# Hybrid decoder block on one core: other PSUM banks for small sums, a third attention head turned through DRAM, a re-ordered output projection and later residual sums

## The chip, the cores and the metric

The kernel runs on one core of one Trainium2 chip. The metric is device time in microseconds (us) of one execution. Before the change it was timed three times: 2241.65, 2243.55 and 2248.02 us, so the median is 2243.55 us. One further execution was recorded by the profiler; every duration below is from that one.

The engines are named as the profile names them: PE is TensorE's matmul unit and PEld its weight load, DVE is VectorE, ACT is ScalarE, POOL is GpSimd, SP is SyncE (which here only issues DMAs). SBUF is the on-chip memory, PSUM the eight accumulator banks that PE writes.

## The reference

One decoder layer over 512 tokens of width 2048, in float32. What matters here:

```
h = rms_norm(x);  parts = h @ w_in
o_nsa = 8 query heads over compressed, selected and window keys   (nsa_mixer)
o_gla = 4 heads of gated linear attention                         (gla_mixer)
x = x + concat(rms_norm(o_nsa), o_gla) @ w_out

cq = rms_norm(per head of rms_norm(x) @ w_cq)      # 4 heads of 128, 512 tokens
ck, cv = the same of the 256 memory tokens
p = softmax(cq @ ck^T);  x = x + (p @ cv) @ w_co   # cross attention

hf = rms_norm(x);  gg, uu = split(hf @ w_gu)
return x + (silu(gg) * uu) @ w_down                # d_ff = 5632
```

## The kernel before, in words

**Precision.** Every float32 operand is split into a high and a low part (`split`, lines 201 to 207: ACT casts the high part, DVE subtracts to get the low one), and each product is three matmuls, high by high, high by low and low by high (`mm3`, which calls the helper that records every matmul at line 110). A weight tile of 128x1024 elements goes from DRAM to a `w` tile and from there to a `wh` and a `wl` tile. A product of full width (512 columns) follows the one before it on PE after about 0.227 us.

**Order of the work.** The program is traced once and a list scheduler at build time fixes the order of every engine's instructions from a model of their times; at run time each engine takes its instructions in that fixed order and waits on semaphores. Work is written as "flows": generators that run beside the big projections. `flows.tick()` is called after every two 128-row steps of a projection (eight times in a projection of 2048 rows), and `yield n` in a flow puts its next piece n ticks later in the program. `behind(i)` forces the instructions inside it to come after instruction i on its engine. PSUM banks are lent by name: `mm` has three buffers, `s` two, `t` two, `o` one. A tile of SBUF that is lent by name waits in the same way until an earlier holder has been read for the last time.

**The eight heads of the first attention** (`nsa_head`, line 926 on). Each head's query projection (`in_tile`) ends in an `mm` bank. The head takes the squares, sums them (`partial_sums` on DVE, four ticks later `total_sums` at line 937, which takes a PSUM bank for one matmul of 16 columns against a matrix of ones and gives it back when DVE has read it), and works out its scale. Then come eight groups of scores, each in an `s` bank: mm3, a DVE reduction over them (line 1017, its running minimum is the tile `mn`) and an exponential on ACT. When they are done, the weights are turned by PE (line 1072) and multiplied with the values into the `o` bank, in two rounds b = 0 and 1. Head 0 is started just before the projection `natural(w_vsw, ...)` of the values, which holds three `mm` banks and the `o` bank from its start to its end (`natural_end`, which reads them out at lines 206 and 207); the other heads run beside the projections that follow.

**Cross attention** (`cross_head`, line 1198 on). Four projections of w_cq follow each other, and head h starts when projection h is done. Two ticks later (one for the last head) its scores are computed against 256 memory tokens in two `s` banks, then scaled and put through the softmax (lines 1229 to 1239). The weights must be turned so that memory tokens lie on partitions. For heads 0 and 1 DVE turns 32x32 blocks of them (line 1245, two instructions of 128x512), POOL stores the result to DRAM in four DMAs (line 1250) and loads it back in the wanted order in two (line 1253). For heads 2 and 3 PE turns them into a `t` bank by eight matmuls of 128 columns (line 1266). Ten (heads 0, 1), four (head 2) or six (head 3) ticks after the softmax the turned weights are split into the tiles PH and PL (one buffer each), and after that six products with the memory's values go to the one `o` bank and are split into the pair `oc[h]`.

**The projection w_co** (line 1285 on). Its first four output tiles, m = 0 to 3, use the three `mm` banks and one `s` bank. `co_part(ps, m, hs)` adds three products for each head in hs. Before the change the loop ran over m outside and heads 0 to 2 inside, waiting at h = 2 for that head's pair; the products of head 3 of all four tiles follow (line 1322), and only then are the output tiles added to x and the rest of w_co computed.

**The down projection** (line 1780 on). Four steps over 22 pairs of 128 rows of w_down each; step 2 has two sets of four accumulators, `banks[0]` in the banks mm, o, t, t and `banks[1]` in s, s, mm, mm. At its end ACT copies `banks[0]` to SBUF (line 1832) and `pending` asks for eight additions on DVE that read `banks[1]` from PSUM (two result blocks, line 1762); they are put at kp = 1 of step 3, ahead of the new accumulators. Twelve more additions (`spread`) follow one to a kp from kp = 3 on, eight of them followed by the store of a piece of the output.

Of the kernel before, what the change touches and what calls it, by code (L numbers as in the profile page):

```python
# [10 lines left out]
F32 = mybir.dt.float32  # L11
# [52 lines left out]
def hybrid_block(ctx: ExitStack, tc: tile.TileContext, x_t, mem_t, sv, cmat, umask, w_a, w_r67, w_v, w_vg, w_v3,  # L64
# [14 lines left out]
    def sb(shape, tag, bufs, dt=F32):  # L79
        return (pool_b if tag in LATE else pool).tile(shape, dt, name=tag, tag=tag, bufs=bufs)  # L80
# [173 lines left out]
    def mm3(ps, lhs, rhs, start, stop, again=False):  # L254
        mm(ps, lhs[0], rhs[0], start=start, stop=False, skip_group_check=again)
        mm(ps, lhs[0], rhs[1], start=False, stop=False, skip_group_check=again)
        mm(ps, lhs[1], rhs[0], start=False, stop=stop, skip_group_check=again)

    def part(pair, a, n):
        return pair[0][:, a:a + n], pair[1][:, a:a + n]  # L260

    def view(t, at, *dims):
        return bass.AP(tensor=t.tensor, offset=t.offset + at, ap=[list(t.ap[0])] + [list(d) for d in dims])
# [74 lines left out]
    def total_sums(dst, part, tag):  # L338
        ps = bank(tag)
        mm(ps[:, :16], every32, part, start=True, stop=True)  # L340
        p4 = part.rearrange("p (i g) -> p i g", g=4)
        V.tensor_mul(p4, ps[:, :16].rearrange("p (i g) -> p i g", g=4),
                     own32[:, None, :].to_broadcast([128, NT, 4]))
        V.reduce_sum(dst, p4, axis=AX.X)
# [581 lines left out]
    def nsa_head(h, ps):  # L926
# [7 lines left out]
        sc, sl, neg, part_, m3 = qt[:, 0:4], qt[:, 4:8], qt[:, 8:12], qt[:, 12:28], qt[:, 28:29]  # L934
        partial_sums(part_, sq, row("n"))
        yield W_SUM + 1
        total_sums(neg, part_, "s")
        V.tensor_mul(neg, neg, rc2)
        inv_rms(sc, neg, 128, sl)
        V.tensor_mul(sc, sc, rc)  # L940
# [257 lines left out]
    def cross_head(h, ps):  # L1198
        q = row("Q", F32R), row("Q", F32R)
        sq = row("n")  # L1200
        S.activation(sq, ps, AF.Square)
        split(*q, ps, g_cq)
        cf = triple("cf")
        sc, tmp, v = cf[:, 0], cf[:, 1], cf[:, 2]
        if h < 3:
            part_ = small("qs", 2)[:, :16]
            partial_sums(part_, sq, row("n"))
        yield 1 if h == 3 else 2
        if h == 3:
            pn = bank("t")  # L1210
            for i in range(NT):
                mm(pn[:, i:i + 1], sq[:, 128 * i:128 * i + 128], one, start=True, stop=True)
        scores = [bank("s") for _ in range(2)]
        for a in range(2):
            for i in range(2):
                mm3(scores[a][:, MEM * i:MEM * i + MEM], part(q, 128 * (2 * a + i), 128), part(ckp, MEM * h, MEM),
                    start=True, stop=True)
        if h < 3:
            total_sums(v, part_, "t")
        V.tensor_mul(v, v if h < 3 else pn[:, :NT], rc[1])  # L1220
        inv_rms(sc, v, 128, tmp)
        V.tensor_mul(sc, sc, rc[0])
        sm, mn = triple("sm"), triple("mn")
        halves = []
        for a in range(2):
            s = scores[a]
            p = row("e")
            two = slice(2 * a, 2 * a + 2)
            V.tensor_reduce(mn[:, 0, two], s.rearrange("p (i n) -> p i n", i=2), axis=AX.X, op=OP.max, negate=True)
            V.tensor_mul(mn[:, 0, two], mn[:, 0, two], sc[:, two])  # L1230
            for i in range(2):
                j = 2 * a + i
                S.activation(p[:, MEM * i:MEM * i + MEM], s[:, MEM * i:MEM * i + MEM], AF.Exp,
                             bias=mn[:, 0, j:j + 1], scale=sc[:, j:j + 1], accum_out=sm[:, 0, j:j + 1])
            V.reciprocal(mn[:, 1, two], sm[:, 0, two])
            for i in range(2):
                j = 2 * a + i
                pi = p[:, MEM * i:MEM * i + MEM]
                V.tensor_scalar(pi, pi, mn[:, 1, j:j + 1], None, op0=OP.mult)
            halves.append(p)  # L1240
        rows = []
        if h < 2:
            z = sb([128, 1024], "w", 4)
            for a in range(2):
                V.transpose(view(z, 64 * a, (32, 2), (128, 8), (1, 32)), halves[a])
            d = dram.tile([128, 1024], F32, name="crossp", tag="crossp", bufs=2)
            dv = d.rearrange("(c s) (b a x) -> s b c a x", s=32, b=2, a=4)
            zv = z.rearrange("p (b c x) -> p b c x", b=2, c=4)
            for a in range(4):
                G.dma_start(dv[:, :, :, a], zv[32 * a:32 * a + 32])  # L1250
            for b in range(2):
                rows.append(row("st"))
                G.dma_start(rows[b], d[:, 512 * b:512 * b + 512])
        yield 6 if h == 3 else 10 if h < 2 else 4
        pts = []
        for b in range(2):
            pt = sb([128, 1280], ("PH", "PL")[b], PTB, F32R)
            pts.append((pt[:, :512], pt[:, 512:1024]))
            if rows:
                split(*[view(t, 0, (32, 4), (128, 4), (1, 32)) for t in pts[b]],  # L1260
                      rows[b].rearrange("p (a i x) -> p a i x", a=4, i=NT))
                continue
            tp = bank("t")
            for i in range(NT):
                c = MEM * (i % 2) + 128 * b
                PE.transpose(tp[:, 128 * i:128 * i + 128], halves[i // 2][:, c:c + 128], ident)
            split(*pts[b], tp)
        yield 2 if h == 3 else 1
        o = bank("o")
        for b in range(2):  # L1270
            mm3(o, part(cvp[b], 128 * h, 128), pts[b], start=b == 0, stop=b == 1)
        pair = row(OC[h], F32R), row(OC[h], F32R)
        split(*pair, o)
        oc.append(pair)
# [9 lines left out]
    sb([128, 24], "pad", 1)  # L1284
    co = [Weights(w_co[c], 1024, ahead=60) for c in range(2)]
    ps4 = [bank("mm") for _ in range(3)]
    for m in range(4):
        if m == 3:
            ps4.append(bank("s"))
        for h in range(3):  # L1290
            flows.until(lambda: len(oc) > h)
            co_part(ps4[m], m, (h,))
            flows.tick()
    flows.drain()
# [489 lines left out]
    for step, plan in enumerate(STEPS):  # L1784
        rs_ = range(len(plan))
        for kp in range(NK):
            if step or kp % 2 == 0:
                load_w(step, kp)

            if kp == 1:  # L1790
                for s in pending:
                    gather_all(s)
                if step == 0:
                    banks[0] = banks[1]
                elif step == 2:
                    banks[1] = [bank(t) for t in SETS[1]]
                else:
                    banks = [[bank(t) for t in SETS[r]] for r in rs_]
            if kp in (1, NK - 1):
                for r in rs_ if kp == 1 else reversed(rs_):  # L1800
                    for x in range(4):
                        for k in (kp - 1, kp):
                            down_product(step, r, k, (x,))
                        if step == 3 and kp == NK - 1:
                            gather(ADD, *((0, 0), (1, 0))[r], banks[r], x, True)
            elif 1 < kp < NK - 2:
                for r in rs_:
                    down_product(step, r, kp, range(4))
            if kp in ROWS[step]:
                load_rows(*ROWS[step][kp])  # L1810
            if kp in SUMS[step]:
                add_rows(*SUMS[step][kp])
            if step == 0 and kp == 3:
                last_turn = turn(hs, NB - 1)
            if kp >= 3 or step:
                for go in last_turn.get(NK * step + kp, ()):
                    go()
            move_h(step, kp)
            if step == 3 and kp > 2 and spread:
                with behind(*last_split):  # L1820
                    gather(*spread.pop(0))
        if step == 0:
            pending = [(COPY, 0, 1, banks[0])]
            res[0, 1] = new_res(0, 1)
        elif step == 1:
            pending = [(COPY, 0, 0, banks[0]), (COPY, 1, 1, banks[1]), (ADD, 0, 1, banks[1])]
            for a in range(2):
                res[a, a] = new_res(a, a)
        elif step == 2:
            u = quarters(sb2("H"))  # L1830
            for x in range(4):
                S.copy(u[x], banks[0][x])
            pending = [(SUB, 1, 1, banks[1]), (ADD, 1, 0, banks[1])]
            spread = [(*p, x, last) for *p, last in ((SUB, 1, 1, u, True), (SUB, 0, 1, u, True), (ADD, 1, 0, u, False))
                      for x in range(4)]


_OUT = (4, 128, 2048)
# [120 lines left out]
```

## Time and profile before

| | |
|---|---|
| three timed executions | 2241.65, 2243.55, 2248.02 us |
| profiled execution, its own time | 2241.54 us |
| its span, first to last instruction | 2239.8 us |
| granted TensorE clock | 1.000 |
| PE, PEld busy | 2229.3 us, 1851.8 us |
| DVE, ACT, POOL busy | 1709.5 us, 1159.6 us, 299.7 us |
| mean DMA throughput | 200 GB/s |

The profile's page gives busy time by engine, the chain of waits that ended last, and groups of instructions by line. The trace behind it can be asked for windows (busy time and number of instructions, in brackets behind an x, of each engine in a stretch), for waits (who waited for whom), for a timeline of one engine, and for DMAs with their time from issue to landing. Times are counted from the first instruction. PE's matmuls are pipelined and their ends are modelled: the distance between two starts says how long PE was held, and the time in square brackets behind a row is idle time before it with the instruction that ended it.

### The profile page before, as it was taken

How to read it: one execution, taken by the hardware profiler on the slowest of the kernel's cores; microseconds unless marked ns; L12 is line 12 of the kernel's file. 1: busy time of each engine (PE TensorE's matmuls, PEld its weight loads, DVE VectorE, ACT ScalarE, POOL GpSimd, SP SyncE). 2: the span in 40 equal slices, each digit the busy share in tenths (PEclk: the TensorE clock that was granted, in tenths of full speed). 3: DMA queues.
4: the chain of work that ended last, by engine and by line, in shares of the span. 5: the costliest groups of instructions: out<-in, count | busy, mean ns of one | idle time of the engine just before them, and what ended most of it. 6: DMA issues, size and time to landing. Idle time of an engine off the chain costs nothing.

```text
span 2239.8 us, 29015 instructions
## 1 busy us (share of the span) xinstructions
PE 2229.3 (100%) x10404; PEld 1851.8 (83%) x10404; DVE 1709.5 (76%) x2653; ACT 1159.6 (52%) x1715; POOL 299.7 (13%) x453
## 2 busy tenths in 40 slices
PE   9999999999999999999999999999999999999999
PEld 8898888888887888888888888888888888888887
DVE  7648986667878336788889888988888886766786
ACT  7534564556777324575455445544554554454443
POOL 0122221122221220120011101110110011001000
PEclk9999999999999999999999999999999999999999
DMA  8588778965563983595456546554664477768684
GB/s 305 179 220 201 190 188 223 248 172 170 151 169 112 250 229 95 162 265 201 148 184 197 173 150 195 189 170 154 198 201 142 150 281 261 268 241 281 250 278 163
DMA packets 130784, 448.23 MB, mean 200 GB/s; under 512 B 16240, under 2 KB 17520, under 8 KB 127696
## 3 DMA queue, kind: packets, MB, share of 16 engines
q1 hardware_dynamic: 81040, 304.71, 39.8%
q0 software_dynamic: 47152, 137.39, 24.7%
q10 hardware_dynamic: 2448, 4.28, 0.5%
q8 instruction: 81, 1.33, 0.2%
q14 instruction: 63, 0.52, 0.1%
HBM read 401.10 MB, written 107.09 MB: 227 GB/s over the span
## 4 chain that ended last, share of the span: by engine, by line
PE 96%; DVE 2%; DMA 1%; ACT 1%; issue 1%; SPq 0%; DVEq 0%; POOLq 0%; ACTq 0%
PE mm L110 52%; PE t L110 18%; PE s L110 14%; PE o L110 11%; PE t L1072 1%; DMA raw<-gu 0%; DMA raw<-td 0%; DMA PH<-w_ck 0%; DMA ss<-q 0%; DMA ss<-KV 0%; DVE ql L204 0%; DVE e L741 0%; DVE P L1017 0%; DVE wl L204 0%; ACT wh L204 0%
## 5 line engine op out<-in xcount | busy, mean ns | idle before, releaser
L204 ACT CAST qh<-raw 128x1024 fp32r<-128x1024 f32 (+1 forms) x494 | 478.5, 976 | 468.2 <-PE o L110 128.0
L204 DVE TENSOR_TENSOR ql<-raw,qh 128x1024 fp32r<-128x1024 f32 (+1 forms) x494 | 550.6, 1124 | 106.1 <-PE mm L110 40.1
L110 PE MATMUL mm<-X,wh 128*128 128x512 f32 x1664 | 524.4, 394 | 0.0
L110 PEld LDWEIGHTS mm<-X,wh 128*128 128x128 f32 x1664 | 306.4, 188 | 59.1 <-issue 0.8
L110 PE MATMUL t<-qh,PB 128*128 128x512 f32 x968 | 333.0, 389 | 0.0
L110 PE MATMUL mm<-X,wl 128*128 128x512 f32 x832 | 325.6, 392 | 0.5 <-DVE wl L204 0.5
L110 PE MATMUL mm<-qh,PB 128*128 128x512 f32 x868 | 309.1, 389 | 0.1
L204 DVE TENSOR_TENSOR wl<-w,wh 128x1024 fp32r<-128x1024 f32 (+2 forms) x172 | 205.5, 1200 | 130.8 <-ACT wh L204 127.9
L204 ACT CAST wh<-w 128x1024 fp32r<-128x1024 f32 (+2 forms) x172 | 176.8, 1033 | 232.9 <-PE mm L110 151.8
L110 PE MATMUL s<-qh,PB 128*128 128x512 f32 x672 | 231.0, 389 | 0.0
L110 PE MATMUL mm<-qh,PA 128*128 128x512 f32 x640 | 220.0, 389 | 0.0
L110 PEld LDWEIGHTS t<-qh,PB 128*128 128x128 f32 x968 | 181.7, 188 | 37.9
L110 PEld LDWEIGHTS mm<-qh,PB 128*128 128x128 f32 x868 | 163.0, 188 | 34.2 <-ACT qh L204 0.7
L110 PE MATMUL t<-ql,PB 128*128 128x512 f32 x484 | 188.3, 389 | 0.0
L110 PE MATMUL o<-qh,PB 128*128 128x512 f32 x484 | 187.4, 389 | 0.0
L110 PEld LDWEIGHTS mm<-X,wl 128*128 128x128 f32 x832 | 156.2, 188 | 33.9 <-DVE wl L204 1.8
L110 PE MATMUL mm<-ql,PB 128*128 128x512 f32 x434 | 169.3, 390 | 1.1 <-DVE ql L204 1.1
L110 PEld LDWEIGHTS s<-qh,PB 128*128 128x128 f32 x672 | 126.1, 188 | 25.9
L110 PEld LDWEIGHTS mm<-qh,PA 128*128 128x128 f32 x640 | 120.1, 188 | 25.0
L110 PE MATMUL s<-ql,PB 128*128 128x512 f32 x336 | 131.0, 390 | 0.1
L110 PE MATMUL mm<-ql,PA 128*128 128x512 f32 x320 | 124.5, 389 | 0.0
L1424 DVE TENSOR_TENSOR raw<-raw 128x1024 f32<-128x1024 f32 x80 | 97.0, 1223 | 18.8 <-DMA raw<-w_gu 18.4
(534 smaller groups left out, 3493.4 us busy)
## 6 DMA issues: line engine op xcount, KB each, us to landing
raw<-w_gu SPq DMA_DIRECT2D x80, 768.0 KB, 4.2
raw<-w_down SPq DMA_DIRECT2D x88, 512.0 KB, 4.8
raw<-w_gu SPq DMA_DIRECT2D x80, 512.0 KB, 3.6
td<-w_down POOLq DMA_DIRECT2D x66, 512.0 KB, 7.4
w<-w_a SPq DMA_DIRECT2D x60, 512.0 KB, 6.3
raw<-td SPq DMA_DIRECT2D x22, 1024.0 KB, 6.7
w<-w_out SPq DMA_DIRECT2D x32, 512.0 KB, 6.1
HR<-h POOLq DMA_DIRECT2D x28, 512.0 KB, 4.5
```

What stands on the lines that cost most here:

```text
L110: last_mm[0] = PE.matmul(*args, **kw)
L204: last_split[:] = S.copy(hi, src), V.tensor_sub(lo, src, hi)
L1072: PE.transpose(tp[:, 128 * (i - j):128 * (i - j) + 128], ps_[b][:, POFF[i] + 128 * j:POFF[i] + 128 * j + 128], ident)
L1424: V.tensor_add(raw[:, 0:1024], raw[:, 0:1024], raw[:, 512:1536])
```

## The change

There are four edits.

1. `nsa_head`: the small sums' matmul takes an `mm` bank, no longer an `s` bank.
2. `cross_head`: the score matmuls are put behind the matmul last recorded before them; head 2 is turned as heads 0 and 1 are, with nine ticks to its split; and for all three heads the way through DRAM is cut into two halves of 128 memory tokens each: two DVE instructions of 128x256 into a 512 wide tile (`q1` or `rs` in place of a `w` tile), four stores and one load for each half, all eight stores ahead of the two loads.
3. `w_co`: the first four tiles' products go head by head, heads outside and tiles inside.
4. Down projection: at the end of step 2 ACT also copies `banks[1]` to SBUF, nothing is pending at step 3, and the eight additions that read those banks join `spread`, which begins at kp = 1 and has twenty entries; the eight that are followed by a store come at kp = 9 to 16.

```
@@ nsa_head
-        total_sums(neg, part_, "s")
+        total_sums(neg, part_, "mm")
@@ cross_head
-        for a in range(2):
-            for i in range(2):
-                mm3(scores[a][:, MEM * i:MEM * i + MEM], part(q, 128 * (2 * a + i), 128), part(ckp, MEM * h, MEM),
-                    start=True, stop=True)
+        with behind(last_mm[0]):
+            for a in range(2):
+                for i in range(2):
+                    mm3(scores[a][:, MEM * i:MEM * i + MEM], part(q, 128 * (2 * a + i), 128), part(ckp, MEM * h, MEM),
+                        start=True, stop=True)
...
-        if h < 2:
-            z = sb([128, 1024], "w", 4)
-            for a in range(2):
-                V.transpose(view(z, 64 * a, (32, 2), (128, 8), (1, 32)), halves[a])
-            d = dram.tile([128, 1024], F32, name="crossp", tag="crossp", bufs=2)
-            dv = d.rearrange("(c s) (b a x) -> s b c a x", s=32, b=2, a=4)
-            zv = z.rearrange("p (b c x) -> p b c x", b=2, c=4)
-            for a in range(4):
-                G.dma_start(dv[:, :, :, a], zv[32 * a:32 * a + 32])
+        if h < 3:
             for b in range(2):
-                rows.append(row("st"))
-                G.dma_start(rows[b], d[:, 512 * b:512 * b + 512])
-        yield 6 if h == 3 else 10 if h < 2 else 4
+                z = row(("q1", "rs")[b])
+                for a in range(2):
+                    V.transpose(view(z, 64 * a, (32, 2), (128, 4), (1, 32)),
+                                view(halves[a], 128 * b, (MEM, 2), (1, 128)))
+                d = dram.tile([128, 512], F32, name="crossp", tag="crossp", bufs=6)
+                for a in range(4):
+                    G.dma_start(d[:, 128 * a:128 * a + 128].rearrange("(c s) x -> s c x", s=32),
+                                z[32 * a:32 * a + 32].rearrange("s (c x) -> s c x", c=4))
+                rows.append(d)
+            for b in range(2):
+                t = row("st")
+                G.dma_start(t, rows[b])
+                rows[b] = t
+        yield 6 if h == 3 else 10 if h < 2 else 9
@@ w_co
-    for m in range(4):
-        if m == 3:
-            ps4.append(bank("s"))
-        for h in range(3):
-            flows.until(lambda: len(oc) > h)
+    for h in range(3):
+        flows.until(lambda: len(oc) > h)
+        for m in range(4):
+            if len(ps4) == m:
+                ps4.append(bank("s"))
             co_part(ps4[m], m, (h,))
             flows.tick()
@@ down projection
-            if step == 3 and kp > 2 and spread:
+            if step == 3 and kp and spread:
...
-            pending = [(SUB, 1, 1, banks[1]), (ADD, 1, 0, banks[1])]
-            spread = [(*p, x, last) for *p, last in ((SUB, 1, 1, u, True), (SUB, 0, 1, u, True), (ADD, 1, 0, u, False))
-                      for x in range(4)]
+            w = [sb2("PA") for _ in range(4)]
+            for x in range(4):
+                S.copy(w[x], banks[1][x])
+            pending = []
+            spread = [(*p, x, last) for *p, last in ((SUB, 1, 1, w, False), (ADD, 1, 0, w, False), (SUB, 1, 1, u, True),
+                                                     (SUB, 0, 1, u, True), (ADD, 1, 0, u, False)) for x in range(4)]
```

## The prediction, made before the changed kernel was run

> **What bounds the kernel now.** I read the page first, its busy times and the chain of waits:
>
> ```profile
> PE 2229.3 (100%) x10404; PEld 1851.8 (83%) x10404; DVE 1709.5 (76%) x2653; ACT 1159.6 (52%) x1715; POOL 299.7 (13%) x453
> ...
> PE 96%; DVE 2%; DMA 1%; ACT 1%; issue 1%; SPq 0%; DVEq 0%; POOLq 0%; ACTq 0%
> ```
>
> PE bounds the kernel: 96% of the chain that ended last is matmuls. So an edit can win only the holes in PE's row, and it can lose as much as it opens. Busy time hides small holes, because the ends of matmuls are modelled; so I read windows next, for the number of matmuls in the bracket behind PE (first column), then PE's own waits in the three stretches that are touched (360 to 720, 870 to 1010, 1980 to 2240 us):
>
> ```profile
> 448.00:504.00 56.00, 56.00 (x289) 47.43 (x288) 37.94 (x112) 32.03 (x67) 12.86 (x17) 1.00 0.67 171
> 1064.00:1120.00 56.00, 56.00 (x248) 46.36 (x247) 48.44 (x60) 25.22 (x30) 4.33 (x7) 1.00 0.43 148
> 2072.00:2128.00 56.00, 55.13 (x244) 45.33 (x243) 39.98 (x39) 27.66 (x30) 5.34 (x10) 1.00 0.69 250
> ```
> ```profile
> PE s L110 <- DVE mn L1017: 1.0, 4, 0.2
> ```
> ```profile
> PE s L110 <- ACT Q L206: 0.8, 1, 0.8
> ```
> ```profile
> PE mm L110 <- DVE ql L204: 0.9, 1, 0.9
> ```
>
> A stretch of full-width matmuls alone holds 248 in 56 us, 0.226 us each. In the row from 1064 on there is no hole at all; the down projection's 244 is four short, 0.9 us. The three touched stages show waits of 1.0, 0.8 and 0.9 us. That is the purse: a few microseconds of 2240. About 0.3%, 6.7 us, is what a measurement of this kernel can tell from no change, so the prize lies below it, and the question is whether an edit opens a hole larger than that.
>
> **Edit 1, the sums' bank.** The wait on `mn` is the sums' matmul standing for an `s` bank:
>
> ```profile
> 543.06 0.27 PE L110 MATMUL o<-PL,KV 128*128 128x128 f32 x1
> 543.18 0.27 PE L110 MATMUL o<-PH,KV 128*128 128x128 f32 x1
> 543.70 0.37 PE L110 MATMUL s<-qs,every 128*128 128x16 f32 x2 [0.25 <-DVE mn L1017]
> ```
>
> The product at 543.18 holds PE some 0.12 us, as its like at 543.06 did, so 0.40 us are lost. The waits view has four such; a fifth, smaller, without a hole in the busy row I put at 0.2. In an `mm` bank they vanish, since beside one projection in progress and one just read out the third is free: 4 x 0.40 + 0.2 = **1.8 us won**. The transposes behind it and the next scores find their bank at the same time as now, so no wait takes their place for sure (rival 3 prices that).
>
> Head 0 is different. Its sums run while the value projection holds all three `mm` banks:
>
> ```profile
> 388.69 0.29 PE L110 MATMUL s<-qs,every 128*128 128x16 f32 x2
> ...
> 449.70 0.60 PE L1072 MATMUL t<-ident,P 128*128 128x128 f32 x4
> ```
> ```profile
> 436.66 0.75 DVE L207 SCALAR_TENSOR_TENSOR KV<-mm,rc,KV 128x512 fp32r<-128x512 f32 x1
> ```
> ```profile
> 405.44 0.41 DVE L998 TENSOR_SCALAR P<-P,cf 128x384 f32<-128x384 f32 x1
> ```
>
> The sums now come when the first of these banks is read out, about 436.7, 48 us later; head 0's eight groups of scores follow them. Its first round is scaled at 405.9 now, 17.2 us after the sums; at that pace it would be ready at 453.9, 4.2 us after the turning at 449.70 wants it. That pace is set by ticks; without them the groups run as fast as DVE and ACT let them, and the projections of head 1 give PE other work. So 0 to 4.2 us are lost; below nothing there is no reason. I take **1.0**, near the lower end, because DVE has room there (37.94 of 56 us busy from 448 on). Edit 1 is worth -1.8 + 1.0 = -0.8 us.
>
> **Edit 2 and 3, the scores' place.** Head 1's scores stand in front of a projection that was ready:
>
> ```profile
> 894.14 0.61 PE L110 MATMUL mm<-X,wh 128*128 128x512 f32 x2
> 895.57 0.51 PE L110 MATMUL s<-P,Q 128*128 128x256 f32 x2 [0.81 <-ACT Q L206]
> ```
>
> Two products of 0.227 end at 894.59, so 0.98 us are lost. Behind the twelve matmuls recorded before them, 2.7 us of work, the scores come when Q is there: **1.0 us won**, at least 0.5 if the matmuls themselves wait for their weights.
>
> **The third head.** Removed are eight turning matmuls:
>
> ```profile
> 923.00 0.70 PE L1266 MATMUL t<-ident,e 128*128 128x128 f32 x4
> 923.46 0.48 PE L110 MATMUL mm<-X,wl 128*128 128x512 f32 x1
> ```
>
> Four take 0.46, all eight 0.9 us of PE. The way through DRAM takes their place. The rows of heads 0 and 1 give its price:
>
> ```profile
> 906.68 0.70 DVE L1245 STREAM_TRANSPOSE w<-e 128x512 f32<-128x512 f32 x1
> 907.30 0.65 DVE L204 TENSOR_TENSOR PL<-st,PL 128x512 fp32r<-128x512 f32 x1
> ...
> 923.58 0.62 DVE L1239 TENSOR_SCALAR e<-e,mn 128x256 f32<-128x256 f32 x2
> ...
> 948.06 0.42 DVE L1349 TENSOR_TENSOR PB<-PB 128x256 f32<-128x256 f32 x1
> ```
> ```profile
> DMA to landing us min/median/max: 2.4/3.9/4.7
> ```
> ```profile
> crossp<-w POOLq DMA_DIRECT2D x8, 128.0 KB, 3.7
> st<-crossp POOLq DMA_DIRECT2D x4, 256.0 KB, 4.5
> ```
> ```profile
> 907.67 2.46 POOL L1250 DMA_DIRECT2D crossp<-w  x4 [6.84 <-DVE w L1245]
> 914.17 1.11 POOL L1253 DMA_DIRECT2D st<-crossp  x2 [4.04 <-DMA crossp<-w]
> 944.53 0.55 POOL L1389 DMA_DIRECT2D ss<-rs  x1 [29.25 <-ACT rs L1387]
> ```
>
> Head 2's softmax ends at 923.58 + 0.62 = 924.2. Two of the four new transposes, at 0.42 each (the price of a DVE pass over 128x256; the row is another operation, and I take it as the nearest), must be done before the first store: 925.0, and 0.3 to the issue (from 906.68 + 0.70 to 907.67): 925.3. Eight stores at 0.62 (a quarter of 2.46) follow each other on POOL, on which nothing else is queued there: the last is issued at 929.6. In head 1 the load came 4.6 us after its last store's issue (907.67 + 2.46 - 0.6 = 909.5, to 914.17): here 934.2. It lands 4.5 us later, 938.7. Then come the casts:
>
> ```profile
> 904.85 0.62 ACT L204 CAST PH<-st 128x512 fp32r<-128x512 f32 x1
> ```
> 0.62 and 0.65 (that of 907.30) to both parts of the second half, 940.0; the last two products with the values, 0.45: 940.4; 0.6 for the high part of head 2's pair: 941.0, and 0.7 for the low one: 941.7 (like casts and subtractions). Before, this pair was there when its products were wanted, and those of head 3 ended the first four tiles just before the fifth began:
>
> ```profile
> 942.44 0.61 PE L110 MATMUL mm<-M,wh 128*128 128x512 f32 x2
> ```
>
> Now twelve products of head 2 and, on the same accumulators, twelve of head 3 come after 941.0: 24 x 0.227 = 5.4, and 0.5 for the low part that is late: 946.9. That is 4.5 us behind 942.44. What covers the round trip is head 3's own work and the 24 products of heads 0 and 1, which edit 3 puts ahead; all of it is done some 5 us too soon, and no other product can start, as the rest of w_co needs those four banks and both heads. Heads 2 and 3 also share PH, PL and the one `o` bank, so whichever comes second adds up to 1.5; the stores carry half the bytes of before, which may save up to 1 at each of two landings. Range 2.5 to 6, taken **4.7**, a little of that sharing in it; nothing below zero, unless the landings are the shortest (rival 2). Heads 0 and 1 pay the same trip with a projection over them: nothing. The wait of the loads behind eight stores keeps nobody else: no other DMA is on POOL's queue until 944.
>
> [...]
>
> **Edit 4.** DVE's additions from PSUM stand in front of a low part that PE waits for:
>
> ```profile
> 2114.19 1.28 DVE L1762 TENSOR_TENSOR T<-T,mm 128x512 f32<-128x512 f32 x2
> 2115.38 2.36 DVE L204 TENSOR_TENSOR ql<-raw,qh 128x1024 fp32r<-128x1024 f32 x2
> ```
> ```profile
> 2115.40 0.39 PE L110 MATMUL o<-qh,PB 128*128 128x512 f32 x1
> 2116.66 0.50 PE L110 MATMUL mm<-ql,PB 128*128 128x512 f32 x1 [0.87 <-DVE ql L204]
> ```
>
> 2116.66 - 2115.63 = 1.03 us. With the two additions gone the low part is there 1.28 us sooner: **1.0 won**. The four copies cost ACT 4 x 0.6, where it is half idle (27.66 of 56 above), and the eight additions go one to a pair of rows, where DVE has 16 us free in 56; nothing, or 0.3 if one meets a late split. Later stores still end long before the last pair.
>
> **Sum.** -0.8 - 1.0 + 4.7 - 1.0 = **+1.9 us**. The profiled execution took 2241.54, 2.0 under the median of 2243.55 and at the lowest of the three. 2243.4 by its scale, 2245.4 by the median's: I give 2244.5.
>
> **Rivals.** (1) Slower: the order on PE is fixed at build. If head 2's products with the values are put where the text has them, between those of w_co for heads 0 and 1, PE stands in front of them until 940.4, with 12 products of head 1, head 3's turning and its own products still behind: 12 + 12 + 12 + 3 + 6 products of 0.227 and 0.9 make 11.1, so 951.5 to 952, 9 to 9.5 us behind 942.44 and 4.6 above my term. It decides from a term of 9.5 on (1.9 - 4.7 + 9.5 = 6.7). Total +6.5 to +7: about 2250. For it: the place in the text. Against it stands the group of the products with the values:
>
> ```profile
> L110 PE MATMUL o<-PH,st 128*128 128x512 f32 x12 | 4.7, 447 | 0.1
> ```
>
> Those of the two heads that go by DRAM now were put where the data was there: 0.1 us of idle time. (2) The round trip at its shortest: landings of 2.4 each, as the quickest row has it, save 1.3 and 2.1, so the term is 1.3 and the total -1.5: 2241. For it: half the bytes. Against: the medians. (3) Edit 1 does not do what it says: the next scores take up the wait for the same DVE pass, or head 0's full 4.2 us come through to the end. Total +3.7 to +5.1: about 2249.
>
> **Chances.** Forecast 0.50, shortest trip 0.20, no gain in edit 1 0.13, PE in front of head 2 0.17. Only the last crosses 6.7 us, and barely, with some of the third beside an unlucky measurement: slower 0.17. Faster needs 6.7 us where all waits together are under 4 and the turning 0.9: 0.05. Same 0.78. The range takes the shortest trip without a price for head 0 (-2.5 on the lowest run: 2239) less 1.5 for the spread of runs, and at the upper end rival 1 and 1 us of spread: 2237.5 to 2251.
>
> **What would show it.** Right: no `s<-qs,every` in heads 1 to 7 with an idle time before it; head 0's sums near 437; no idle time before head 1's scores; some 5 us of idle PE between 928 and 942, ended by the pair of head 2; the products of w_co for head 2 starting near 940 (all after the 1 or 2 us won before them); no wait on `ql` near 2116. Wrong: no hole there, or landings under 3 us; or more than 4 us lost between 437 and 720.

## The result, and the profile after

The changed kernel is slower: a median of 2265.54 us in five executions (2265.08 to 2268.55), against 2242.50 for the kernel before in five. The ratio is 1.0102, with a 95% interval of 1.0088 to 1.0116. That is 23 us lost where the prediction had a small loss of 2 inside a range of 2237.5 to 2251.

The page of the changed kernel, its busy times and its chain:

```profile
span 2266.6 us, 29056 instructions
...
PE 2234.9 (99%) x10396; PEld 1856.2 (82%) x10396; DVE 1710.9 (75%) x2661; ACT 1161.5 (51%) x1719; POOL 309.0 (14%) x471
...
PE 94%; DVE 2%; DMA 2%; ACT 1%; issue 1%; POOL 0%; SPq 0%; DVEq 0%; POOLq 0%; ACTq 0%
```

PE's busy time is 5.6 us longer for eight matmuls less, and the span is 26.8 longer. So PE stood idle for some 21 us more, and some of its work ran slower. The windows say where. First the kernel before, then the changed one (columns: stretch, length, busy time of PE, PEld, DVE, ACT and POOL with the number of instructions, granted clock, DMA share, GB/s):

```profile
392.00:448.00 56.00, 55.97 (x284) 46.35 (x283) 39.06 (x90) 30.65 (x53) 10.94 (x16) 1.00 0.91 248
```
```profile
392.00:448.00 56.00, 47.29 (x221) 38.01 (x221) 21.21 (x39) 18.13 (x26) 7.99 (x10) 0.96 0.83 213
448.00:504.00 56.00, 46.35 (x224) 38.18 (x223) 35.96 (x99) 27.26 (x59) 8.50 (x12) 0.86 0.51 128
```

Two neighbouring windows hold 221 and 224 matmuls instead of 284 and 289, a loss that no other window of a touched stage comes near. PE's waits in this stretch of the changed kernel (time in total, times, longest); the kernel before has none here:

```profile
PE t L110 <- ACT Q L204: 8.6, 1, 8.6
PE s L110 <- DVE mn L1017: 6.5, 2, 6.3
PE mm L110 <- ACT wh L204: 2.3, 2, 1.1
PE t L110 <- DVE Q L204: 0.8, 1, 0.8
```

Their places on PE's timeline:

```profile
440.46 0.31 PE L110 MATMUL mm<-qs,every 128*128 128x16 f32 x2
...
447.40 2.06 PE L110 MATMUL s<-KS,Q 128*128 128x416 f32 x6 [6.31 <-DVE mn L1017]
449.69 3.87 PE L110 MATMUL s<-KV,Q 128*128 128x128 f32 x12 [0.23 <-DVE mn L1017]
462.17 0.48 PE L110 MATMUL t<-wl,Q 128*64 128x256 f32 x1 [8.61 <-ACT Q L204]
```

Head 0's sums come at 440.46, near where the prediction had them (436.7). But they are not followed by other work of PE: only by holes of 6.3 and 8.6 us. The matmul that waits in the second hole is not of head 0 at all. `t<-wl,Q` belongs to the compress units of the value branch (`compress_unit`, the weights w_c1 against gathered blocks of the values), whose last two in the kernel before ran at 424 to 439, before head 0's turning.

What they waited for shows on POOL. The kernel before:

```profile
408.10 0.61 POOL L113 DMA_DIRECT2D pcd<-pcz  x1
414.60 1.66 POOL L113 DMA_DIRECT2D e<-pcd  x3 [5.88 <-ACT wh L204]
...
416.98 1.04 POOL L817 MEMSET e<- 128x512 f32 x1
```

The changed kernel, and behind it its DVE and its ACT:

```profile
455.78 0.61 POOL L113 DMA_DIRECT2D pcd<-pcz  x1 [17.75 <-DVE pcz L973]
458.36 1.66 POOL L113 DMA_DIRECT2D e<-pcd  x3 [1.97 <-DMA pcd<-pcz]
460.01 0.54 POOL L817 MEMSET e<- 128x512 f32 x1
463.03 0.53 POOL L817 MEMSET e<- 128x512 f32 x1 [2.48 <-DVE Q L204]
```
```profile
460.58 1.04 DVE L823 TENSOR_TENSOR e<-KV,vecs 128x248 f32<-128x248 f32 x2 [1.90 <-POOL e L817]
```
```profile
461.71 0.71 ACT L204 CAST Q<-e 128x256 fp32r<-128x256 f32 x2 [4.75 <-DVE e L823]
```

Read it upwards. PE waits for ACT's split of a block into `Q`; ACT for DVE's gathering of that block (line 823); DVE for POOL's zeroing of the tile `e` that holds it (line 817). The zeroing stands behind head 0's loads `e<-pcd`. These wait for the store `pcd<-pcz`, and POOL stood 17.75 us in front of that store until DVE had turned head 0's compressed weights (`pcz`), at the end of head 0's late softmax. In the kernel before the same sequence ran 43 us earlier and cost PE nothing. The tile `e` has two buffers, and they are lent to head 0 and to the blocks in turn.

The rest of the change went much as forecast. The product with the compressed values (`vc`) of head 0 and of head 7, in the kernel before and in the changed one:

```profile
467.82 0.40 PE L110 MATMUL o<-e,vc 96*128 96x512 f32 x1
...
696.72 0.47 PE L110 MATMUL o<-e,vc 96*128 96x512 f32 x1 [0.17 <-DVE e L1058]
```
```profile
497.84 0.40 PE L110 MATMUL o<-e,vc 96*128 96x512 f32 x1
...
723.88 0.48 PE L110 MATMUL o<-e,vc 96*128 96x512 f32 x1 [0.20 <-DVE e L1058]
```

At head 0 the changed kernel is 30.0 us late, at head 7 27.2: heads 1 to 7 won 2.9. Of the 30.0, 5.0 stand there already at 300 us, ahead of all that the change touches (the first `t<-wh,Q` starts at 304.40 instead of 299.38). PE's waits between 168 and 224 us, before and after, hold most of them:

```profile
PE s L110 <- DVE e L741: 0.2, 1, 0.2
```
```profile
PE s L110 <- DVE e L741: 4.1, 2, 3.9
```

This wait of the linear attention, near 190 us, stands at 0 to 4 us in the profiled executions of the runs below, those with edit 1 and those without it. The recorded execution of the changed kernel has it and was also the longest of the five, 3.0 over their median. So the account is: 25.0 lost in the value branch, 2.9 won in the heads, 1.0 won by the scores' place, 1.1 lost by the third head, 0.5 won in the down projection. That is 21.7 us. With the 5.0 of the early stretch it comes to 26.7, where the two spans differ by 26.8; the 23.0 between the medians are 1.3 more than it explains.

### The profile page after: what moved, and what is told of

Same layout as the page of the kernel before. It is cut to its first block, busy times and chain, and to the rows that moved or that the text cites. A ratio compares the mean times of both kernels' runs of the same rounds, so it can differ in the third digit from the quotient of the medians.

```text
span 2266.6 us, 29056 instructions
## 1 busy us (share of the span) xinstructions
PE 2234.9 (99%) x10396; PEld 1856.2 (82%) x10396; DVE 1710.9 (75%) x2661; ACT 1161.5 (51%) x1719; POOL 309.0 (14%) x471
## 4 chain that ended last, share of the span: by engine, by line
PE 94%; DVE 2%; DMA 2%; ACT 1%; issue 1%; POOL 0%; SPq 0%; DVEq 0%; POOLq 0%; ACTq 0%
PE mm L110 51%; PE t L110 18%; PE s L110 14%; PE o L110 11%; PE t L1072 1%; DMA KV<-Q 0%; DVE wl L204 0%; ACT wh L204 0%; DMA raw<-td 0%; DMA raw<-gu 0%; DVE ql L204 0%; DMA ss<-q 0%; DMA PH<-w_ck 0%; DVE e L741 0%; DMA ss<-KV 0%
```

## The experiments

**Theory T**: the loss is all edit 1's, all of it head 0's, and the link is the tile `e`. **Rivals**: the other edits take part in it; or the link is another one, the four buffers of `Q` (some held by head 0) or the `mm` banks, one of which is lent to the sums.

### 1. Edit 1 alone, and all but edit 1

The kernel before with

```
-        total_sums(neg, part_, "s")
+        total_sums(neg, part_, "mm")
```

> The kernel before with edit 1 alone (sums of squares of all heads in an mm bank). Theory T: the whole loss is head 0's sums coming 52 us late; through the rotating tile e they hold up the compress blocks of the value branch, PE runs dry between 425 and 470 us. The changed kernel lost 23 us net; the scores' place won 1.0 there, the third head cost 1.1, the down projection won 0.5, so edit 1 alone costs 23 + 1.0 - 1.1 + 0.5 = 23.4: 2266 us against 2242.5, with head 0's sums near 440 and holes of 6 and 9 us in PE between 445 and 472. Rival (the other edits take part in it, for instance because the program's order moves as a whole): clearly less than the full loss, 2245 to 2260.

Measured: 2264.51 us against 2242.66, ratio 1.0100 [1.0086, 1.0114]. The account has 22.1 for this edit (25.0 lost, 2.9 won), and 21.9 are measured. Its waits between 392 and 504 us are the same four rows as above, to the tenth.

The changed kernel with that line put back:

> The changed kernel with the sums of all heads back in the s bank (edits 2 to 4 alone). Theory T: the loss is gone; what is left is -1.0 (scores' place) + 1.1 (third head through DRAM) - 0.5 (down projection) = -0.4: 2242 us against 2242.5. The prediction's own figures for the same three edits, -1.0 + 4.7 - 1.0, would give 2245.2. Rival (other edits take part in the loss): over 2248.

Measured: 2244.36 us against 2242.66, ratio 1.0009 [1.0000, 1.0018]. So edit 1 makes the loss and the others together next to nothing. The median is 2 us over theory T's 2242; the wait at 190 us took 3.5 in this run's profile, and its eleven executions reach from 2242.04 to 2248.68.

### 2. Head 0 alone put back

The changed kernel with

```
-        total_sums(neg, part_, "mm")
+        total_sums(neg, part_, "mm" if h else "s")
```

> The changed kernel with head 0's sums alone back in the s bank, those of heads 1 to 7 in an mm bank. Theory T: only head 0 stands under the value projection; the other heads keep the gain of the changed kernel's heads (2.8 us between head 0's and head 7's last product, of which 1.8 were waits on mn): -0.4 - 1.8 = -2.2, to -3.2: 2239 to 2240.5 us, the fastest of all. Rival (a later head loses too, or the wait on mn is taken up by the next scores): 2242 or more, no faster than with all sums in the s bank.

Measured: 2239.10 us, ratio to the kernel before 0.9987 [0.9978, 0.9996]. The one head that stands under the value projection makes the whole loss; the other seven gain. This kernel is H below.

### 3. A tile of its own for the blocks

The kernel before with edit 1, and in `compress_blocks`

```
-        blk = row("e").rearrange("p (l n) -> p l n", n=64)
+        blk = row("on" if pe == "pe_v" else "e").rearrange("p (l n) -> p l n", n=64)
```

> The kernel before with edit 1, and one more edit: in the value branch the compress blocks are gathered in another tile (that of the GLA stage's on, which is idle at this time) instead of the rotating tile e of two buffers. Head 0's sums are late as in the changed kernel. Theory T: tile e is the link; with a tile of its own the value branch's compress units run at their old place (424 to 439), PE stays fed, and the loss falls from 23 to between 0 and 6 us: 2242 to 2248 us. Rival Q (two of the four tiles of weights' transposes or splits held by head 0 are the link) and rival B (the mm banks themselves, one now lent to the sums): the loss stays at 15 us or more, over 2257.

Measured: 2242.14 us, ratio 0.9998 [0.9989, 1.0007]: 22 us of edit 1's loss are gone, though head 0's sums still come at 433.87 us. POOL's timeline and the windows of this run:

```profile
387.62 0.99 POOL L817 MEMSET on<- 128x512 f32 x1
...
453.35 0.58 POOL L113 DMA_DIRECT2D pcd<-pcz  x1 [0.82 <-DVE P L998]
455.84 1.67 POOL L113 DMA_DIRECT2D e<-pcd  x3 [1.91 <-DMA pcd<-pcz]
```
```profile
392.00:448.00 56.00, 55.93 (x281) 46.02 (x280) 29.62 (x56) 25.77 (x43) 8.50 (x10) 1.00 0.91 251
448.00:504.00 56.00, 55.41 (x285) 46.23 (x284) 43.24 (x147) 36.06 (x80) 13.19 (x20) 1.00 0.64 166
```

Head 0's loads are as late as in the changed kernel, but nothing of the value branch stands behind them: the third block is zeroed at 387.62, and both windows are nearly full again. `Q` and the `mm` banks are shared here exactly as in the changed kernel, so those rivals fall.

Does the tile gain something by itself? A control, the same edit in the fastest version (experiment 5), where head 0's sums are early:

> The fastest version so far (head 0's sums in the s bank, third head turned by PE, 2238.1 us) with the value branch's compress blocks in a tile of their own: a control for the run in which that tile took the loss away. There is no PE hole between 400 and 500 us in this version, so the tile by itself should bring nothing: 2237.5 to 2238.7 us. If it is faster by more than 1 us, part of what the tile brought in the other run was its own gain and not the end of the wait.

Measured: 2237.87 us, 4.7 under the kernel before on the same chip; without the tile it was 2238.12, 5.0 under the kernel before on its chip. The tile gains nothing that can be told apart.

### 4. Is it the tile, or POOL's order?

The tile of its own also let POOL zero the blocks ahead of the loads. To tell the two apart, edit 1 with the zeroing on another engine:

```
-        G.memset(blk, 0.0)
+        (V if pe == "pe_v" else G).memset(blk, 0.0)
```

> The kernel before with edit 1 (2264.5 us without more), the zeroing of the value branch's compress blocks moved from POOL to DVE; they stay in the rotating tile e. In the runs with all sums in the mm bank POOL zeroes the third block right behind the three loads of head 0's compressed weights, which wait for its late softmax. Theory E (the two buffers of e are lent in the program's order, so a block that comes after head 0's load must wait for it, on whatever engine it is zeroed): PE's holes of 6.6 and 9 us stay, 2262 to 2267 us. Rival P (only POOL's fixed order held the zeroing up): the third block is there near 390 and the loss is gone as with a tile of its own, 2242 to 2246.

Measured: 2264.01 us, ratio 1.0099 [1.0084, 1.0115]. DVE's timeline, and POOL's:

```profile
453.13 0.48 DVE L817 MEMSET e<- 128x512 f32 x1
...
456.18 0.48 DVE L817 MEMSET e<- 128x512 f32 x1 [0.17 <-DVE Q L204]
```
```profile
453.37 1.92 POOL L113 DMA_DIRECT2D e<-pcd  x3 [1.87 <-issue]
```

Off POOL's queue the zeroing is still 65 us later than in a tile of its own. PE's two long waits are 6.3 and 6.6 us. So POOL's queue isn't what holds it. Nor does the block wait for head 0's loads, as the words of theory E have it: it is zeroed 0.24 us before they are issued. It has no idle time before it either, so it stands in its place in DVE's fixed order, behind head 0's softmax. Nor does head 0 sit on the buffer that the blocks take. In the changed kernel the first two blocks are read for the last time at 405.6, so that both buffers are free from then on, and head 0's weights are read only after the fourth block has been zeroed (463.03):

```profile
405.18 0.42 DVE L204 TENSOR_TENSOR Q<-e,Q 128x256 fp32r<-128x256 f32 x1
```
```profile
487.36 0.62 ACT L1051 CAST e<-e 96x512 fp32r<-96x512 f32 x1
```

What is left is the turn: head 0 stands before the last two blocks in the order in which `e` is lent, and the build gives the blocks a place that fits this order, on whatever engine they are zeroed. This follows from experiments 3 and 4 together; the build's own reasons are in no trace, and a third buffer for `e` was not tried.

### 5. The third head

H with the third head turned by PE again:

```
-        if h < 3:
+        if h < 2:
...
-        yield 6 if h == 3 else 10 if h < 2 else 9
+        yield 6 if h == 3 else 10 if h < 2 else 4
```

> The fastest version so far (the changed kernel with head 0's sums in the s bank, 2239.1 us, here called H) with the third head turned by PE again, the other two by DRAM, the order of w_co head by head. In H's profile PE stands idle 1.49 us before the fourth tile's s bank and 0.84 us before head 2's pair; the turning that was taken off PE is worth 0.9. Theory T1 (the trip through DRAM sets both holes): they close, -2.3 + 0.9 = -1.4: 2237.7 us. Rival (the 1.49 us is the order's, since the fourth tile's bank is wanted before head 3's exponentials have let it go): that hole stays or grows, the pair's 0.84 goes and 0.9 of turning comes: 2239.2. By the prediction's 4.7 for this step it would be 2234.4.

Measured: 2238.12 us, ratio to the kernel before 0.9977 [0.9968, 0.9985]. Both holes are gone from PE's waits between 890 and 990 us: products of head 2 (`mm<-on`, from 928.58 us on) now fill the time before the fourth tile's bank. By the medians the third head's way through DRAM costs 1.0 us, or 1.5 when each version is taken against the kernel before on its own chip (H ran on another one); the spread of the executions is larger than that. By the trace it is 1.4 (2.3 of holes, less 0.9 of turning), not 4.7. This version, with head 0's sums and the third head as before, is the fastest together with the control of experiment 3, which cannot be told from it: 5.0 us under the kernel before on the same chip, 27 under the changed one.

H with the old order of w_co:

```
-    for h in range(3):
-        flows.until(lambda: len(oc) > h)
-        for m in range(4):
-            if len(ps4) == m:
-                ps4.append(bank("s"))
+    for m in range(4):
+        if m == 3:
+            ps4.append(bank("s"))
+        for h in range(3):
+            flows.until(lambda: len(oc) > h)
```

> H with the three heads' part of w_co tile by tile again (as in the kernel before), the third head by DRAM as in H. The prediction let the products of heads 0 and 1 for all four tiles (24 x 0.227) cover head 2's trip. Tile by tile, only those of the first tile, 6, stand ahead of head 2's first; the other 18, 4.1 us, come behind. Theory T2: they no longer cover, PE's idle time before head 2's pair grows by 4.1 less the 1.49 of the s bank, which is then wanted later: +2.6: 2241.7 us. Rival (other work fills the place, as head 3's products do now): no more than +0.5, 2239.6.

Measured: 2239.40 us against H's 2239.10. Theory T2 is wrong. PE's two holes are the same, to 0.01 us, and the products of heads 0 and 1 for all four tiles stand ahead of head 2's here too: the list scheduler had put them there whatever the text said. Edit 3 changes next to nothing.

H with head 2's trip in the old form (one tile `w`, four stores, two loads together):

```
+        if h == 2:
+            z = sb([128, 1024], "w", 4)
+            for a in range(2):
+                V.transpose(view(z, 64 * a, (32, 2), (128, 8), (1, 32)), halves[a])
...
+            for a in range(4):
+                G.dma_start(dv[:, :, :, a], zv[32 * a:32 * a + 32])
+            for b in range(2):
+                rows.append(row("st"))
+                G.dma_start(rows[b], d[:, 512 * b:512 * b + 512])
```

> H with head 2's trip in the form of the kernel before: one tile, four stores of 128 KB, two loads of 256 KB together behind all of them. Theory T3 (the trip is shorter than predicted because of its form: stores of 64 KB, and each half's load alone behind its own half's stores): landings return to about 3.7 and 4.5, the second load lands 0.8 to 2 us later after the first store's issue than in H (10.5 us from first store to last landing there), and the time rises by as much: 2240 to 2241. Rival (the landings are short because little else moves at this place): store landings stay near 2.0 to 3.3 and the loads' near 3.0, and with four stores less to issue the trip is 1 to 2 us shorter: 2238 to 2239.

Measured: 2241.48 us (2238.57 to 2247.31) against H's 2239.10 (2237.90 to 2243.40). The executions overlap; the trace is plainer. The DMA view between 948 and 960 us of the changed kernel (KB each, median time from issue to landing), then between 922 and 938 us of this run:

```profile
st<-crossp POOLq DMA_DIRECT2D x2, 256.0 KB, 3.0
crossp<-q POOLq DMA_DIRECT2D x4, 64.0 KB, 2.0
crossp<-rs POOLq DMA_DIRECT2D x4, 64.0 KB, 2.7
```
```profile
crossp<-w POOLq DMA_DIRECT2D x4, 128.0 KB, 3.5
st<-crossp POOLq DMA_DIRECT2D x2, 256.0 KB, 5.8
```

From the first store's issue to the last load's landing it takes 14.7 us in the old form and 10.5 in H, a larger difference than the 0.8 to 2 that theory T3 expected. PE's holes before head 2's products in w_co grow from 2.3 to 4.7. So the form, with what it brings along, makes the short trip. Whether by the smaller stores, by loads that don't fly together, or by fewer weights in flight at that time (3.17 MB moved in those 16 us, 1.66 in the changed kernel's 12) isn't separated.

### 6. The down projection alone

The kernel before with edit 4, that is

```
-            pending = [(SUB, 1, 1, banks[1]), (ADD, 1, 0, banks[1])]
...
+            for x in range(4):
+                S.copy(w[x], banks[1][x])
+            pending = []
```

and the later `spread`:

> The kernel before with the down projection's part of the change alone. The prediction put it at -1.0: 2241.7 us, no hole before ql near 2116. Theory T4: DVE, no longer busy with the two additions (1.28 us), waits for the load of the raw weights instead, so that a hole of 0.4 to 1.1 us is left: -0.6 to 0, 2242.1 to 2242.7 us; the trace tells, the time hardly.

Measured: 2240.82 us against 2243.15, ratio 0.9992 [0.9983, 1.0001]. PE's wait, and DVE ahead of it:

```profile
PE mm L110 <- DVE ql L204: 0.4, 1, 0.4
```
```profile
2113.97 1.23 DVE L1708 TENSOR_TENSOR raw<-raw 128x1024 f32<-128x1024 f32 x1 [1.45 <-DMA raw<-td]
2115.11 1.22 DVE L204 TENSOR_TENSOR PB<-HR,PB 128x1024 fp32r<-128x1024 f32 x1
2116.25 2.35 DVE L204 TENSOR_TENSOR ql<-raw,qh 128x1024 fp32r<-128x1024 f32 x2
```

The two additions are gone from here, and half of the wait stays: DVE now stands 1.45 us until the raw weights land (0.45 in the kernel before, whose additions came behind). T4 holds in the trace; the time is 2.3 us lower, more than the trace explains, but its interval reaches up to no change at all. In the other executions profiled with edit 4 this wait of PE is 0 to 0.4 us six times, but 1.0 in that of experiment 1 with the sums put back, where DVE stood 2.05 us for the raw weights. Without edit 4 it is 0.9 to 1.2. So what the edit wins hangs on when these weights land.

## Why the prediction was wrong

**What bounds the kernel** was right: PE, with a few microseconds in its holes. The best version won 5 us, about the size of the purse.

**Edit 1, head 0: the step that failed.** The prediction followed one line: sums late, scores late, turning at 449.70 late. It wrote "the projections of head 1 give PE other work", and from that "0 to 4.2 us are lost", of which it took 1.0. It never asked who comes after head 0's flow while that is late. Head 0 borrows one of two buffers of `e` for its compressed weights, and the value branch's last two blocks come behind it in the order in which these are lent. So the other work of PE waited as well, and the loss was 25 us. With the blocks in a tile of their own (experiment 3) the prediction's line is all that is left: head 0's first product comes at 469.36 instead of 467.82, 1.5 us late, inside its 0 to 4.2. The trace of before gave a sign of the link: the zeroing at 416.98 comes soon behind head 0's loads on POOL. The prediction read POOL's queue for the third head, where it moved DMAs, and not for head 0, where it moved only a time.

**Where the 25 us went.** By the distances between starts, PE's five holes take some 19 us (the four rows of waits say 18.2). Most of the rest is the clock. The changed kernel's windows at a finer pitch:

```profile
440.00:444.00 4.00, 1.09 (x6) 0.60 (x4) 3.11 (x7) 2.37 (x5) 0.00 (x0) 0.88 0.30 98
444.00:448.00 4.00, 0.59 (x2) 0.61 (x3) 2.64 (x17) 2.72 (x8) 0.00 (x0) 0.50 0.42 131
448.00:452.00 4.00, 3.77 (x15) 3.34 (x14) 2.77 (x17) 3.85 (x11) 0.00 (x0) 0.50 0.01 4
...
464.00:466.00 2.00, 2.00 (x11) 1.90 (x9) 1.55 (x4) 1.79 (x3) 0.00 (x0) 0.50 0.00 0
...
468.00:470.00 2.00, 2.00 (x16) 1.90 (x15) 1.21 (x2) 1.41 (x2) 0.55 (x1) 1.00 0.81 256
```

Behind each of the two long holes the granted clock is 0.50. Behind the second, PE's products of 256 columns start every 0.21 us from 463.22 to 465.78, and every 0.12 us from 467.70 to 469.22, where the clock is 1.00. Between 444 and 468 PE is busy for 10.9 us (the busy times of this view, those of the rows left out included), some 10 of them at a clock of 0.50, so about 4.5 us are lost to it; 19 and 4.5 make 23.5 of the 25. The 4.5 is an estimate from these windows and starts, not tried by itself. The clock itself, read in windows of 0.2 us of the changed kernel: the holes of 1.1 us left the clock at 1.00. In the two long ones (6.3 and 8.6 us) it fell to 0.50 some 2.0 and 3.1 us after PE's last work, and it came back 5.9 us after the work at 447.40 began and 4.8 after that at 462.17.

**Edit 1, heads 3 to 7**: right in sign, and larger: 2.9 us over heads 1 to 7, against 1.8. The distance from head to head fell by 0.6 (33.6 to 33.0), not by the 0.40 read from one spacing.

**The scores' place**: right, 1.0. Head 1's scores in the changed kernel have no wait ahead of them or between them:

```profile
924.26 1.73 PE L110 MATMUL s<-P,Q 128*128 128x256 f32 x12
```

The changed kernel's delay is 27.2 us at head 0's scores and 26.3 at head 2's.

**The third head**: the mechanism was right in part, the size not. The hole before head 2's pair was forecast. The larger one, before the fourth tile's `s` bank, was not: PE stands there until head 3's exponentials have read that bank, with no product of head 2 ready to fill the time:

```profile
PE s L110 <- ACT e L1234: 1.3, 1, 1.3
PE mm L110 <- ACT on L204: 0.7, 1, 0.7
```

The changed kernel's delay grows from 26.3 us at head 2's scores to 27.4 at the first product of the fifth tile (942.44 before, 969.79 now), so the term was 1.1 by the trace; experiment 5 has 1.0 to 1.5, and the sum had 4.7. The mis-sized parts are the landings: I put 4.5 for the load and 4.6 from the last store's issue to the loads', from rows of the old form, where the new form has 3.0 and 3.9, and eight issues of 0.55 instead of 0.62. Together 13.4 us of trip became 10.6, which takes 2.8 of the 4.7 away; the rest of the difference is not worked out:

```profile
948.67 2.20 POOL L1251 DMA_DIRECT2D crossp<-q  x4 [6.00 <-DVE q L1247]
950.86 2.17 POOL L1251 DMA_DIRECT2D crossp<-rs  x4
953.60 0.56 POOL L1256 DMA_DIRECT2D st<-crossp  x1 [0.57 <-ACT cf L302]
956.41 0.56 POOL L1256 DMA_DIRECT2D st<-crossp  x1 [2.25 <-DVE cf L307]
```

The first half's load leaves while the second half's stores are still flying. Rival 2, the shortest trip (term 1.3), was the case that came nearest. The medians from issue to landing were, in the changed kernel, 2.0 and 2.7 us for the stores of 64 KB and 3.0 for the loads, in the old form 3.5 for the stores of 128 KB and 5.8 for the loads (experiment 5).

**Edit 3 as cover** ("24 products of heads 0 and 1, which edit 3 puts ahead") fell: these products do stand ahead, but the order on PE was the scheduler's, with edit 3 or without it. Rival 1, PE in front of head 2's products with the values for 9 us, did not happen: they start at 960.04 us in the changed kernel without a wait.

**Edit 4**: 0.5 instead of 1.0, and nothing in one of the profiled executions. The additions went, and the next to be late was a DMA; the prediction had looked no further than DVE's own instructions.

**Rival 3** had the right place, head 0, but took 4.2 as the full price. Of the signs of being wrong that the prediction named, the one for this place ("more than 4 us lost between 437 and 720") came true. The chance of 0.17 for slower came mostly from rival 1, which played no part.

## What to carry to other kernels

Before a step is made late, list what its flow borrows or has still to borrow (tiles, banks, a place in an in-order queue) and who is next in line for each, even where a buffer stands free: the price of lateness is often paid by work that does not read the result at all. A cover ("PE has other work") is to be named instruction by instruction, and each of these followed back to its own inputs. If one instance out of eight runs under another stage's conditions, give it its own choice: the same edit lost 25 us in head 0 and won 3 in the seven others.

## What the runs showed of the hardware

In the changed kernel two holes of PE cost more than their length: behind those of 6.3 and 8.6 us the matmuls ran at a granted clock of 0.50, which by estimate took about 4.5 us more, while holes of 1.1 us (two, near 427 and 434 us) left it at 1.00. In the wait near 190 us of the same kernel a hole of 3.9 us was followed by a clock of 0.50 from 190.5 to 193.9 us.

A way through DRAM cut into halves (64 KB stores, each load alone behind its own half) took 10.5 us from first issue to last landing (H) where the whole one took 14.7 at the same place (experiment 5), although it issues twice as many stores, at 0.55 us each on POOL against 0.62.
